# A hybrid attention block: the input projection as fp16 halves with scales made on the chip

## The chip, the cores and the metric

The kernel runs on one core of one Trainium2 chip. The metric is the device time of one execution in microseconds, as the median of several runs; an execution is also profiled, and its trace gives the span from the first to the last instruction and the place of each instruction on each engine: PE (TensorE), DVE (VectorE), ACT (ScalarE), POOL (GpSimd) and SP (SyncE, which here issues DMAs). PEld is the loading of PE's weights.

## The reference

One layer of a decoder block on 16 meta tokens and 512 real ones, width 1024, all in float32. Two attention branches of 16 heads each, MLA and forgetting attention ("fox"), read one common input projection:

```
u = rmsnorm(h, pre_norm_g)
cq, ckv, k_pe_raw, z_mla, fq, fk, fv, f_logit, z_fox, gate_a, gate_b = split(u @ w_in)
q  = rmsnorm(cq) @ w_uq ; kv = rmsnorm(ckv) @ w_ukv ; rope on q_pe and k_pe
o_mla = causal_attention(q_m, k_m, v_mla)
cum = cumsum(log_sigmoid(f_logit + fox_forget_b))
o_fox = causal_attention(fq, fk, fv, cum)          # logit[t,s] += cum[t] - cum[s]
y_mla = (o_mla * silu(z_mla)) @ w_br_mla ; y_fox = (o_fox * silu(z_fox)) @ w_br_fox
mixed = (sigmoid(gate_a) * y_mla + sigmoid(gate_b) * y_fox) @ w_out
out = h + rmsnorm(mixed, post_norm_g)              # without the meta tokens
```

## The kernel before

**Split products.** A float32 product is made of three matmuls in the type fp32r: high times high, high times low, low times high. Each operand X is split into a high part (a cast, on ScalarE) and a low part (X minus the high part, on GpSimd or VectorE). `passes` issues the three for each slice of 128 of the contraction. The normed input, transposed, stands in `uTh` and `uTl`.

**Units.** The input projection is cut into units of 128 output columns: q, k and v of a pair of fox heads (PE's fq, fk, v), z of each branch, and the gates (pg). A unit of 512 tokens is 24 matmuls of 512 columns; k and v, with the meta tokens, are 48 matmuls, 24 of 272 and 24 of 256 columns. The weights of a unit come by one DMA of 512 KB into `wraw` (`wload`), are split by `wsplit` (the cast is L136; the low part L105, on the engine that `low[0]` names, mostly GpSimd) and go to PE. `weights` returns the getter, `ahead` ties the load of a unit to a place some units earlier.

**Stages.** The opening (0 to 59 us) norms and transposes the input, makes the small latent projection (psm), q and k of the first fox pair, the rotary part (ppe), v and half a gate. Sixteen attention stages follow, for each of eight pairs of heads first fox, then MLA. A stage on PE is: scores (st), the product of the stage before with its values (ov), and a fill of projection units for later stages. A fox stage fills with z of fox, then z of MLA in three pieces, with the MLA query and key-value units (mq, mk, v from the latents, fp32r) between the pieces; an MLA stage fills with fq, fk and v of the next fox pair. While PE runs the fill, VectorE evicts the scores with the bias and the running maximum (L795; for fox with `cbp` and its masked copy `cbm`, which come back by DMA from `c_dram`, the scan of the forget gates), ScalarE takes exponentials (L830) and makes the high part of the normed probabilities (L865), VectorE their low part (L869), GpSimd the short meta part (L850 to L855), all into `pn`. A transposing DMA brings `pn` to `pt`, and `ov` uses `pt` with the values, in fp16, two heads side by side. The last stage fills with three gates. A merge follows (407 to 490 us: fox's branch product as a Strassen-like set x, y, z, with two gates between its sets), then MLA's branch product (py) with the last gate, the output projection and the norm.

**Order.** PE's order in the attention stages is written by hand in the fills. The other engines take their instructions in the order of a scheduler that goes by priority and dependence; `tc.issue_after` and `keep_in_program_order` pin some of them.

Of the kernel before, what the change touches and what calls it, by code (L numbers as in the profile page):

```python
# [11 lines left out]
F32 = mybir.dt.float32  # L12
# [26 lines left out]
SC_FOX = 1.0 / math.sqrt(HD)  # L39
# [8 lines left out]
ROW = 64  # L48
# [7 lines left out]
def block_kernel(ctx: ExitStack, tc: tile.TileContext, x, meta_tokens, pre_norm_g, w_in, fox_forget_b,  # L56
# [19 lines left out]
    uT0 = [const.tile([128, KD, ROW + L - META], F32R, tag=n, name=n) for n in ("uTh", "uTl")]  # L76
    uTh, uTl = (t[:, :, ROW - META :] for t in uT0)
# [29 lines left out]
    def wload(srcs):  # L107
# [3 lines left out]
        raw = wp.tile([128, 1024], F32, tag="wraw", name=f"wraw{u}")  # L111
# [13 lines left out]
    low = [nc.gpsimd]  # L125

    def room_of(u, up=0):
        w = wp.tile([128, 2112], F32R, tag="w", name=f"w{u}")
        return [w[:, o + up : o + up + 1024] for o in (0, 1024)]

    def wsplit(ld, up=0):

        u, raw, parts, n = ld
        wh, wl = room_of(u, up)
# [9 lines left out]
    def weights(srcs, wrap, up=0):  # L144
# [11 lines left out]
        return get  # L156

# [23 lines left out]
    def unit(name, getw, act, nk, sls, done, banks=None):  # L181
# [26 lines left out]
        if hasattr(getw, "load"):  # L208
            out[0][1].load = getw.load
        return out  # L210
# [5 lines left out]
    def u_act(k):  # L216
        return uTh[:, k, :], uTl[:, k, :]
# [7 lines left out]
    def win_w(off, i, up=0):  # L225
        return weights(lambda: [win[:, :, off + 128 * i : off + 128 * i + 128]], lambda w: by_k(w[0], KD), up)
# [14 lines left out]
    def hl_done(key, n, w):  # L241

        def done(i, ps):
# [6 lines left out]
            with tc.high_priority(offset=30), tc.issue_after(normed[0]) if key == ("q", 0, 0) else nullcontext():  # L250
                halved[key, i] = nc.scalar.copy(hl[:, 0, o : o + w_], ps).ins
            with tc.high_priority(offset=30):
                lowered[key, i] = split_lo(nc.vector, hl[:, 1, o : o + w_], ps, hl[:, 0, o : o + w_]).ins
        return done

    def q_fox(pr):
        return unit(f"fq{pr}", win_w(O_FQ, pr), u_act, KD, REAL, hl_done(("q", 1, pr), S, S))

    def k_fox(pr):
        return unit(f"fk{pr}", win_w(O_FK, pr, UP), u_act, KD, ALLT, hl_done(("k", 1, pr), L, HALF), keybank[0])  # L260
# [4 lines left out]
    with ExitStack() as ph:  # L265
# [56 lines left out]
        fT = pal.tile([NH, L], F32, tag="fT", name="fT")  # L322
# [4 lines left out]

        hns, sts, pts0, squared = {}, {}, {}, {}
# [58 lines left out]

        psms = {}
# [14 lines left out]
        def back(t):  # L403
# [19 lines left out]
            for a, b, i in both:  # L423
                nc.vector.scalar_tensor_tensor(out=sm[:rows, a:b], in0=psm[:rows, a:b], scalar=st2[:rows, 2 + i : 3 + i],
                                               in1=gq[:rows, a:b], op0=ALU.mult, op1=ALU.mult)
# [27 lines left out]
        tps(gps[:, 0, 0:KD], g8, ident[0:KD, 0:KD])  # L453
        squares(0, pin)
        scaled(0, pin)
        pin(nc.vector.tensor_copy(gcol, gps[:, 0, 0:KD]))
# [943 lines left out]
```

## Time and profile before

| | |
|---|---|
| median of 3 runs | 585.56 us (585.5 to 585.57) |
| the profiled execution | 585.71 us |
| its span | 583.5 us |
| opening | 0 to 59 us |
| 16 attention stages | 59 to 407 us |
| merge with gates | 407 to 490 us |
| branch product of MLA, output projection, norm | 490 to 583.5 us |

The span is shorter than the time of the execution by what lies around the first and the last instruction. The page gives the busy time of each engine, which is an average over these parts; its chain of work goes back from the last instruction to whatever released each step, so that it names what sets the end.

### The profile page before, as it was taken

To read this page: it belongs to the slowest core of one execution; us is meant where nothing else is said; L and a number is where in the kernel's file an instruction comes from. 1 tells how busy PE (TensorE), PEld (TensorE's weight loads), DVE (VectorE), ACT (ScalarE), POOL (GpSimd) and SP (SyncE) were. 2 spreads that over 40 slices of the span, in tenths; PEclk is the share of its full clock that TensorE was granted. 3 is DMA by queue.
4 is the path that set the end of the run, shared out by engine and by line. 5 is a ranking of instruction groups with operands and counts; after the bars stand their busy time and mean duration, and the time that the engine had idled before them with its cause. 6 is when DMAs were issued, how large, how long until landed. Compare 5 with 4: busy or idle time off the path is not lost.

```text
span 583.5 us, 11105 instructions
## 1 busy us (share of the span) xinstructions
PE 574.2 (98%) x3841; PEld 496.5 (85%) x3841; DVE 414.5 (71%) x1156; ACT 356.4 (61%) x816; POOL 200.7 (34%) x270
## 2 busy tenths in 40 slices
PE   8999999999999999999999999999999999999995
PEld 6989889889889888888898898878998998888884
DVE  5854876884775775767758748895747876468967
ACT  7856774884774775767748747944343462443762
POOL 4317835464468472654544634520000000000000
PEclk9999999999999999999999999999999999999999
DMA  9535699999978999988987978977722534332603
GB/s 293 119 88 151 125 189 218 234 184 269 175 167 158 231 192 215 220 164 208 186 175 182 216 158 147 184 168 259 210 73 72 145 105 132 89 110 88 237 0 144
DMA packets 219999, 97.46 MB, mean 167 GB/s; under 512 B 131456, under 2 KB 209672, under 8 KB 219944
## 3 DMA queue, kind: packets, MB, share of 16 engines
q1 hardware_dynamic: 219944, 96.77, 71.2%
q8 instruction: 30, 0.49, 0.3%
q14 instruction: 25, 0.20, 0.1%
HBM read 62.36 MB, written 3.97 MB: 114 GB/s over the span
## 4 chain that ended last, share of the span: by engine, by line
PE 93%; ACT 2%; DMA 2%; issue 1%; POOL 1%; SPq 0%; DVE 0%; DVEq 0%; ACTq 0%; POOLq 0%
PE z L99 17%; PE pg L99 15%; PE v L99 9%; PE fk L99 8%; PE fq L99 8%; PE x L99 8%; PE py L99 7%; PE st L99 7%; PE ov L99 5%; PE psm L99 3%; PE y L99 2%; PE mq L99 2%; DMA pt<-pn 1%; PE ppe L99 1%; DMA wsr<-in_w_in_dram 1%; PE mk L99 1%
## 5 line engine op out<-in xcount | busy, mean ns | idle before, releaser
L105 POOL TENSOR_TENSOR w<-wraw,w 128x1024 fp32r<-128x1024 f32 (+2 forms) x61 | 118.6, 1951 | 113.8 <-ACT w L136 81.5
L136 ACT CAST w<-wraw 128x1024 fp32r<-128x1024 f32 (+1 forms) x72 | 74.6, 1041 | 48.5 <-PE py L99 19.7
L99 PE MATMUL z<-uTh,w 128*128 128x512 f32 x256 | 85.0, 393 | 0.0
L99 PE MATMUL pg<-uTh,w 128*128 128x512 f32 x256 | 80.7, 391 | 0.0
L830 ACT ACTIVATE sf<-sf,nb 128x272 f32<-128x272 f32 (+3 forms) x128 | 72.7, 569 | 11.5 <-DVE nb L795 10.6
L105 DVE TENSOR_TENSOR w<-wraw,w 128x512 fp32r<-128x512 f32 (+1 forms) x55 | 51.6, 949 | 27.9 <-ACT w L1125 20.0
L869 DVE SCALAR_TENSOR_TENSOR pn<-sf,ri,pn 128x512 f16<-128x512 f32 (+3 forms) x128 | 69.6, 609 | 1.6 <-ACT pn L865 1.5
L865 ACT ACTIVATE pn<-sf,ri 128x128 f16<-128x128 f32 (+3 forms) x128 | 59.7, 548 | 0.5 <-DVE ri L835 0.5
L99 PEld LDWEIGHTS pg<-uTh,w 128*128 128x128 f32 x256 | 48.1, 188 | 10.2 <-issue 0.3
L99 PEld LDWEIGHTS z<-uTh,w 128*128 128x128 f32 x256 | 48.1, 188 | 10.2
L99 PE MATMUL z<-uTl,w 128*128 128x512 f32 x128 | 50.1, 391 | 0.0
L99 PE MATMUL pg<-uTl,w 128*128 128x512 f32 x128 | 49.9, 390 | 0.0
L99 PE MATMUL fk<-uTh,w 128*128 128x272 f32 (+1 forms) x256 | 48.5, 283 | 0.0
L99 PE MATMUL v<-uTh,w 128*128 128x272 f32 (+1 forms) x256 | 47.5, 283 | 0.0
L99 PE MATMUL fq<-uTh,w 128*128 128x512 f32 x128 | 42.0, 398 | 0.0
L99 PE MATMUL st<-hlk,hlq 64*128 64x272 f32 (+4 forms) x480 | 41.2, 299 | 0.0
L710 DVE TENSOR_REDUCE vsc<-v 128x1 f32<-128x272 f32 (+1 forms) x32 | 13.2, 433 | 39.5 <-PE v L99 39.5
L99 PEld LDWEIGHTS fk<-uTh,w 128*128 128x128 f32 x256 | 40.4, 188 | 0.3
L99 PEld LDWEIGHTS v<-uTh,w 128*128 128x128 f32 x256 | 40.0, 188 | 0.1
L99 PE MATMUL py<-gh,w 128*128 128x512 f32 x128 | 39.7, 389 | 0.0
L99 PEld LDWEIGHTS st<-hlk,hlq 64*128 64x128 f32 x480 | 33.1, 186 | 4.1 <-ACT vh L729 2.8
L99 PE MATMUL v<-uTl,w 128*128 128x256 f32 (+1 forms) x128 | 36.2, 283 | 0.0
(255 smaller groups left out, 1332.1 us busy)
## 6 DMA issues: line engine op xcount, KB each, us to landing
wraw<-in_w_in_dram SPq DMA_DIRECT2D x56, 512.0 KB, 4.8
cbp<-c_dram SPq DMA_DIRECT2D x16, 264.0 KB, 4.0
wraw<-in_w_br_fox_dram SPq DMA_DIRECT2D x8, 512.0 KB, 4.2
tb<-in_w_out_dram SPq DMA_DIRECT2D x8, 512.0 KB, 5.4
wraw<-in_w_br_mla_dram SPq DMA_DIRECT2D x8, 512.0 KB, 4.2
wraw<-in_w_out_dram SPq DMA_DIRECT2D x6, 512.0 KB, 4.2
xr<-in_x_dram SPq DMA_DIRECT2D x4, 512.0 KB
out_dram<-yo SPq DMA_DIRECT2D x8, 256.0 KB, 2.0
```

The source lines that it names most:

```text
L99: nc.tensor.matmul(*a, **k)
L105: return eng.tensor_tensor(out=lo, in0=src, in1=f32(hi), op=ALU.subtract)
L136: nc.scalar.copy(wh[:, :n], raw[:, :n])
L710: nc.vector.tensor_reduce(out=sc[:, i : i + 1], in_=ps, op=ALU.max, axis=AX.X, apply_absolute_value=True)
L830: exps[b // 3] = nc.scalar.activation(sf, sf, AF.Exp, bias=sums["nb"][:, h, b : b + 1], scale=-1.0, accum_out=sums["su"][:, h, b : b + 1]).ins
L865: normed[:] = [nc.scalar.activation(hi, sf, AF.Copy, scale=rib).ins]
L869: nc.vector.scalar_tensor_tensor(out=lo, in0=sf, scalar=rib, in1=hi, op0=ALU.mult, op1=ALU.subtract)
```

## The change

All units of the input projection, except the first fox q, k and v and the first gate (`plain_w`), become objects of a class `Halved`: their weights are multiplied by a power of two s per unit and held as two fp16 halves, and the input is held as fp16 halves `hTh`, `hTl` beside `uTh`, `uTl`. PE still does three matmuls for each slice of the contraction. What was scaled is scaled back in the operations that read the result (`.r`: the scale of tanh, of the eviction in `hl_done`, of v's factor `vsc`).

For each unit one instruction takes the largest magnitude of each partition (Abs with a running sum as a bound on ScalarE, L198, or a reduction on VectorE, L200), one stage ahead of the conversion. For each set of two or three units a matmul of 1 to 3 columns with a constant 128x128 tile `spread` brings the sum over partitions to all of them, VectorE cuts it to a power of two and inverts it (L213, L215), GpSimd makes `.r` (L216). The high half is then one activation with a scale (L255), the low half two instructions on GpSimd (L260, L261) or one on VectorE (L258).

```diff
+    def scales(ws):
+        def peak(j):
...
+            if on[0] is nc.scalar:
+                    tc.keep_in_program_order(nc.scalar.activation(junk[0], raw, AF.Abs, accum_out=mp))
+            else:
+                tc.keep_in_program_order(nc.vector.tensor_reduce(out=mp, in_=raw, op=ALU.max, axis=AX.X, apply_absolute_value=True))
+        def run_():
...
+            mm(ps, spread, sc[:, 0:2].bitcast(BF16)[:, 0:n], start=True, stop=True)
...
+                nc.vector.tensor_scalar(out=t.bitcast(I32), in0=ps.bitcast(I32), scalar1=0x7F800000, scalar2=0x00800000,
+                                        op0=ALU.bitwise_and, op1=ALU.bitwise_or)
+                nc.vector.reciprocal(inv, t)
+                nc.gpsimd.tensor_scalar(out=r, in0=t, scalar1=su[:, 5:6], scalar2=1.0, op0=ALU.mult, op1=ALU.mult)
...
+    class Halved:
...
+            room = wp.tile([128, 1088], F32R, tag="w", name=f"w{u}", bufs=4)
+            hi, lo = (room.bitcast(F16)[:, o : o + 1024] for o in (0, 1024))
...
+                self.hi = nc.scalar.activation(hi, raw, AF.Copy, scale=self.s).ins
...
+                if low[0] is nc.vector and not self.pool:
+                    nc.vector.scalar_tensor_tensor(out=lo, in0=raw, scalar=self.s, in1=hi, op0=ALU.mult, op1=ALU.subtract)
+                else:
+                    nc.gpsimd.tensor_scalar(out=raw, in0=raw, scalar1=self.s, scalar2=1.0, op0=ALU.mult, op1=ALU.mult)
+                    self.lo = nc.gpsimd.tensor_tensor(out=lo, in0=raw, in1=hi, op=ALU.subtract).ins
...
     def u_act(k):
-        return uTh[:, k, :], uTl[:, k, :]
+        return hTh[:, k, :], hTl[:, k, :]
...
+        def narrowed(t, after):
...
+            with tc.issue_after(squared[3]):
+                nc.scalar.activation(hTh[:, :, ts], f32(uTh[:, :, ts]), AF.Copy, scale=su[:, 2:3])
...
+                for out, u, op, x in ((rest, uTh, ALU.subtract, hTh[:, ks, ts]), (hTl[:, ks, ts], uTl, ALU.add, rest)):
+                    with tc.issue_after(after):
+                        nc.vector.scalar_tensor_tensor(out=out, in0=f32(u[:, ks, ts]), scalar=su[:, 2:3], in1=x, op0=ALU.mult, op1=op)
...
+        for t in (4, 0, 1):
+            narrowed(t, lowered["sm", 3])
         run(qk[7:])
+        for t in (2, 3):
+            narrowed(t, lowered[("k", 1, 0), t - 2])
...
-                fill = vts[br, pr] + q + k[:KD] + v + k[KD:]
+                    fill = vts[br, pr] + q + k[:KD] + v[:4] + call(ws[0].scale, ws[0]) + v[4:8] + call(lambda n=si + 1: peaks(sets[n][2:], nc.vector)) + v[8:] + call(ws[1]) + k[KD:]
```

Other edits make room: the split weights of what stays fp32r take two tiles (`w`, `wl`) of two pools, loads run through more buffers and further ahead (`wraw2`, `wb`), the tiles of the attention results (`gT`) take the place of `uTh` and `uTl`, the merge gets rooms of its own for the gates' weights, and the second rotary unit stands seven steps later in its fill. In the merge every second gate's low half is made on VectorE.

On PE, a piece of the order in the middle of a fox stage's fill, before. The rows are matmuls of z of fox and the first of mq, the MLA query unit; an fp32r matmul is one instruction with its weights.

```order
L99 MATMUL z_1529<-uTh,w_1524 128x512 x2
L99 MATMUL z_1529<-uTl,w_1524 128x512
L99 MATMUL z_1529<-uTh,w_1524 128x512
L99 MATMUL mq_1593<-cTh,w_1579 128x512
L99 MATMUL mq_1593<-cTl,w_1579 128x512
```

The same fill in the change, at the middle of z of fox and at its end. `spread` and `scale_1658` belong to the scales of the next pair's q, k and v.

```order
L104 LDWEIGHTS spread
L104 MATMUL scale_1658<-sc_1388,spread 128x3
L104 LDWEIGHTS w_1435
L104 MATMUL z_1619<-hTh,w_1435 128x512
...
L104 MATMUL z_1619<-hTh,w_1435 128x512
L104 MATMUL mq_1684<-cTh,w_1679 128x512
L104 MATMUL mq_1684<-cTl,w_1679 128x512
```

Weights of the fp16 units are loaded by instructions of their own, a small matmul with a load of `spread` stands inside z, and where mq begins, fp16 gives way to fp32r, as it does at each border between a z piece and the MLA units.

On POOL, the weights that are split during one fox stage, before (`vsc` is a tiny factor of v):

```order
L105 TENSOR_TENSOR w_1785<-wraw_1527,w_1785 128x1024
L105 TENSOR_TENSOR w_1846<-wraw_1584,w_1846 128x1024
L720 TENSOR_SCALAR vsc_1647<-vsc_1647 128x1
L105 TENSOR_TENSOR w_1900<-wraw_1600,w_1900 128x1024
L850 TENSOR_TENSOR mt_1864<-sf_1681,ri_1679 128x32
```

And in the change, for the same stage:

```order
L216 TENSOR_SCALAR sc_1388<-sc_1388,su 128x3
L260 TENSOR_SCALAR wraw_1091<-wraw_1091,sc_1388 128x1024
L261 TENSOR_TENSOR w_1758<-wraw_1091,w_1758 128x1024
L260 TENSOR_SCALAR wraw_1093<-wraw_1093,sc_1388 128x1024
L261 TENSOR_TENSOR w_1775<-wraw_1093,w_1775 128x1024
L886 TENSOR_SCALAR vsc_1740<-vsc_1740 128x1
L260 TENSOR_SCALAR wraw_1095<-wraw_1095,sc_1388 128x1024
L920 TENSOR_SCALAR vsc_1740<-sc_1385,vsc_1740 128x1
L261 TENSOR_TENSOR w_1932<-wraw_1095,w_1932 128x1024
L1020 TENSOR_TENSOR mt_1965<-sf_1789,ri_1787 128x32
```

Each low half has a pass over the raw weights ahead of its subtraction; the first meta operation of the next stage's probabilities (`mt`) stands behind them as before.

On ACT, the opening from the first high part of q (`hlq`) to the last table load, before. `fa` is the forget gate, the casts into `w` are weights: `w_777` is v of the first pair.

```order
L251 CAST hlq_618<-fq_578 128x512
L520 ACTIVATE fa<-fT 16x528
L136 CAST w_777<-wraw_733 128x1024
L521 ACT_TABLE_LOAD
L521 ACTIVATE fa<-fa 16x528
L251 CAST hlk_651<-fk_626 128x272
L522 ACT_TABLE_LOAD
L522 ACTIVATE fa<-fa 16x528
L251 CAST hlk_651<-fk_654 128x256
```

The same piece in the change, from the input's halves on; v's cast is `w_824` now, and `w_777` is the rotary unit's.

```order
L522 ACTIVATE hTh<-uTh,su 128x8x128 x3
L582 CAST cTh<-pc_616 128x3x128
L583 CAST KPH<-pc_616 32x128
L584 ACTIVATE fT<-pc_616,fb 16x128
L376 ACTIVATE hlq_646<-fq_594,eps_t 128x512
L671 ACTIVATE fa<-fT 16x528
L162 CAST w_777<-wraw_772 128x512
L672 ACT_TABLE_LOAD
L672 ACTIVATE fa<-fa 16x528
L376 ACTIVATE hlk_680<-fk_655,eps_t 128x272
L673 ACT_TABLE_LOAD
L673 ACTIVATE fa<-fa 16x528
```

Behind the last of these rows stand v's cast `w_824` and then the second half of `hlk`. On DVE the fourteen passes of L530 that make `hTl` and its rests stand between the operations of the opening, the last five of 512 elements between the low half of `hlk` and the scan of the forget gates.

More of the change, by code (lines that the diff above doesn't have):

```diff
@@ L985, in block_kernel @@
         lctx.close()
-        gpool = gctx.enter_context(tc.tile_pool(name="gpool", bufs=1, side="right"))
-        gT += [gpool.tile([128, KD, S], F32, tag=n, name=n) for n in ("gT0", "gT1")]
-        run(opening[len(pe0) : -4])
-        behind[:] = [halved[("k", 1, 0), 1]]
+        for w in first_z:
+            w.room = lambda: more[0].tile([128, 1024], F32, tag="wraw2", name=f"wraw{uid[0]}")
+            w.load()
+            w.peak()
+        behind[:] = [squared[3]]
+        run(opening[len(pe0) : len(pe0) + KD])
+        behind[:] = [halved[("k", 1, 0), 1]]
+        g[0][1].prep()
+        first_z[0].scale()
+        first_z[0]()
+        run(opening[len(pe0) + KD : -4])
+        cycle[0] = 7
+        for w in sets[0]:
+            w.load()
         run(opening[-4:])
@@ L1210, in block_kernel @@
             split_to(S2, g11)
[L1211 to L1213 removed]
+            next(pairs[0])
+        run(after[1])
+        with tc.issue_after(sets[-1][1].hi):
             split_to(A12, g12)
```

329 lines of the change are left out of this document (256 added, 73 removed).

## The prediction

> **What bounds the kernel now.** I read the page first: the busy share of each engine, the clock row, and the chain of work that ended last.
>
> ```profile
> PE 574.2 (98%) x3841; PEld 496.5 (85%) x3841; DVE 414.5 (71%) x1156; ACT 356.4 (61%) x816; POOL 200.7 (34%) x270
> PEclk9999999999999999999999999999999999999999
> PE 93%; ACT 2%; DMA 2%; issue 1%; POOL 1%; SPq 0%; DVE 0%; DVEq 0%; ACTq 0%; POOLq 0%
> ```
>
> PE is busy nearly throughout at full clock, and 93% of the chain is PE. Next the waits of PE by what ended them; these are the longest and the last.
>
> ```profile
> PE spun L99 <- DVE KPL L238: 1.4, 1, 1.4
> PE ov L99 <- DMA pt<-pn: 0.3, 1, 0.3
> ```
>
> Both lie early; after the first ov, PE waits for nobody. So a microsecond of stream removed behind that ov is a microsecond of span, as long as no other engine falls behind; and what is removed ahead of it counts only if that ov comes earlier as well. The profiled execution took 585.71 us for a span of 583.5; the 2.2 us around it stay. The median of the three runs, 585.56, is 0.15 us lower, so the sum is made on 585.7 and rounded.
>
> **The stream.** The order of PE gives the matmuls that turn fp16: 912 of 512 columns (z 384, pg 360, fq 168), and 336 each of 272 and of 256 (fk, v). Their pace today, from the chain (start, us, what):
>
> ```profile
> 98.38 2.72 PE fk L99 x24
> 105.25 5.66 PE z L99 x24
> 112.28 2.04 PE z L99 x9
> 130.39 3.04 PE fk L99 x24
> 438.07 10.90 PE pg L99 x48
> ```
>
> 10.90/48 = 227 ns for 512 columns, 3.04/24 = 126.7 for 272, 2.72/24 = 113.3 for 256. What fp16 costs is seen in ov, which runs two heads side by side on 64 columns of weights each. Five narrow windows of PE's timeline in one ov; the first column is the start of the first pair in flight.
>
> ```profile
> 103.67 0.60 PE L99 MATMUL ov<-pt,vp 128*64 128x512 f16 x4
> 103.89 0.55 PE L99 MATMUL ov<-pt,vp 128*64 128x512 f16 x4
> 104.10 0.49 PE L99 MATMUL ov<-pt,vp 128*64 128x384 f16 x4
> 104.70 0.39 PE L99 MATMUL ov<-pt,vp 128*64 128x256 f16 x4
> 104.81 0.39 PE L99 MATMUL ov<-pt,vp 128*64 128x256 f16 x6
> ```
>
> From 103.67 to 104.10 two pairs of 512 start: 215 ns each; the pair of 256 takes 109 or 110. For 272 I interpolate 116. The saving is 912 x 12.1 ns = 11.0 us, 336 x 10.7 = 3.6, 336 x 4 = 1.3 to 1.4: **-16 us**. No full 128-column fp16 weight stands in the trace; if it gave nothing this would be 0, and there is no row by which it would give more.
>
> **Switches and scale matmuls.** fp16 units now alternate with fp32r ones. In a pair of stages z, mq, z, mk, z, mv, z changes type six times (48 in eight pairs), and ppe and the merge add about 18: 66. No row has fp16 beside fp32r in the same tile shape. The nearest are a change of matmul mode in the opening, and the start of z after ov, which changes type and tile.
>
> ```profile
> 36.11 4.80 PE fq L99 x21
> 40.92 0.44 PE pc L102 x4
> 41.35 0.70 PE fq L99 x3
> ```
>
> The 24 fq and 4 pc take 5.94; 24 x 0.227 leaves 0.49 for four 128-column transposes, which alone could fill 0.44: 0.05 per round trip, 0.03 per switch. The upper end is z: 5.66 - 24 x 0.227 = 0.21. So 66 switches cost 0 to 14 us; only the type changes here, so I take 0.03: **+2 us**. The 23 scale matmuls (128x128 weights, 1 to 3 columns) cost between 0 and the 109 ns of 256 columns; half: **+1.3 us**. The start of z after ov may fall too, since both are fp16 now: 0 to -0.2 at each of 15 places; I take 0.
>
> **The helpers inside a pair of stages.** A pair is a fox and an mla stage; this one is typical (the columns are PE, PEld, DVE, ACT, POOL busy):
>
> ```profile
> 228.44:269.25 40.81, 40.81 (x321) 35.43 (x322) 28.69 (x105) 28.13 (x70) 20.66 (x30) 1.00 0.94 206
> L345 ACT ACTIVATE hn<-ht x4: 1044/1060/1062, 6.8 to 17.6; 128x1024 f32<-128x1024 f32 x3, 16x1024 f32<-16x1024 f32 x1
> L345 ACT ACTIVATION_READ_ACCUMULATOR hn<-ht x4: 183/184/187, 7.8 to 18.6; 128x1 f32 x3, 16x1 f32 x1
> L710 DVE TENSOR_REDUCE vsc<-v x32: 423/433/443, 53.6 to 364.8; 128x1 f32<-128x272 f32 x16, 128x1 f32<-128x256 f32 x16
> ```
>
> PE's pair shortens to about 40.81 - 1.6 (48 z and 24 fq at 12.1 ns, 48 at 10.7, 48 at 4) + 0.2 + 0.1 = 39.5. ACT gets two maxima of 1.06 + 0.18: 30.6. The hi conversions replace casts of the same 1024 elements. DVE gets three reductions; 433 ns for 272 elements scales to at most 1.6 for 1024, and four tiny scale operations (0.2 each): 34.4. Both fit. POOL's low halves become two instructions, a TENSOR_SCALAR of 128x1024 (time T) and the old TENSOR_TENSOR; five units a pair, so 5T + about 1.3 for tiny ones: **22 + 5T**. T is not in the trace. Rows near it, with the median or mean in ns:
>
> ```profile
> L306 POOL CAST wsh<-wsr x3: 904/912/962, 8.2 to 10.7; 128x864 fp32r<-128x864 f32 x3
> L523 POOL TENSOR_SCALAR fa<-fT x1: 1994/1994/1994, 42.5 to 42.5; 16x528 f32<-16x528 f32 x1
> L105 POOL TENSOR_TENSOR w<-wraw,w x61: 728/2387/3747, 24.2 to 381.7; 128x1024 fp32r<-128x1024 f32 x43, 128x256 fp32r<-128x256 f32 x16, 128x512 fp32r<-128x512 f32 x2
> L869 DVE SCALAR_TENSOR_TENSOR pn<-sf,ri,pn x128: 344/605/2744, 67.8 to 378.1; 128x128 f16<-128x128 f32 x32, 128x256 f16<-128x256 f32 x32, 128x384 f16<-128x384 f32 x32, 128x512 f16<-128x512 f32 x32
> L869 DVE SCALAR_TENSOR_TENSOR pn<-sf,ri,pn 128x512 f16<-128x512 f32 (+3 forms) x16 | 8.5, 598 | 0.2 <-ACT pn L865 0.2
> ```
>
> One-input CAST: 912 x 1024/864 = 1.1 us. The same operation, but mult then max on 16 partitions: 1994 x 1024/528 = 3.9. I take T near the cast, 1.1 to 1.5, because there too one tensor is read and one written and the width matches; that is a choice between far ends, and the first rival takes the other. POOL is then about 29 of 39.5 and hidden. For engines that all run fuller I add **+1 us** (0 to 5).
>
> [...]
>
> **The opening.** Here PE's stream is not all that counts. ACT must now also make hTh (five operations, 4224 elements a partition, 4.5 us by the 1060 row), ahead of the last cTh; DVE makes hTl in two passes of 8448 elements, some 10 us; and v0's weight cast, which stood ahead of the table loads, stands behind them. Rows of ACT's, POOL's and DVE's timelines and of the chain (start, us):
>
> ```profile
> 41.39 0.48 ACT L438 CAST cTh<-pc 128x384 fp32r<-128x384 f32 x1 [3.00 <-PE pc L102]
> 43.46 1.03 ACT L136 CAST w<-wraw 128x1024 fp32r<-128x1024 f32 x1
> 48.02 0.65 ACT L522 ACTIVATE fa<-fa 16x528 f32<-16x528 f32 x1
> 46.46 2.40 POOL L105 TENSOR_TENSOR w<-wraw,w 128x1024 fp32r<-128x1024 f32 x1
> 50.57 5.77 PE v L99 x48
> 48.57 0.34 ACT L251 CAST hlk<-fk 128x256 fp32r<-128x256 f32 x1
> 48.78 0.70 DVE L524 SCALAR_TENSOR_TENSOR fa<-fa 16x528 f32<-16x528 f32 x1 [1.59 <-ACT fa L522]
> 49.74 1.24 DVE L527 TENSOR_TENSOR_SCAN fa<-fa 16x528 f32<-16x528 f32 x1
> 57.63 0.20 POOL L924 COPY cbm<-cbp 128x16 f32<-128x16 f32 x1 [0.70 <-DMA cbp<-c_dram]
> 60.03 0.31 DVE L795 CUSTOM_DVE_ANT_0 sf<-st,cbp 128x144 f32<-128x144 f32 x1 [0.60 <-PE st L99]
> 74.89 6.82 DMA pt<-pn
> 81.85 2.04 PE ov L99 x26
> ```
>
> hTh fits into the 3.0 idle and a little before, and is about 0.8 late. Without the 1.03 cast but with ppe's 0.6 in its place, Ln ends about 0.4 later than 48.67, so v0's cast ends near 50.1 and POOL's low half near 52.5. PE wants that low half with its third v matmul, at 50.8: a stall of about 1.7. Behind the wait stand pg and the scores. On DVE the scan stands behind four more passes of hTl: hlk's cast (0.34) ends about 50.4, then its low half (0.4), five passes of 512 elements (0.7 each, as L524) and the scan, ending near 55.5 instead of 50.98. Its c goes out by DMA and returns as cbp 6.6 us later, near 62, where the first evictions read cbp at 60.03. They start about 2 to 3 us late; maximum, pn, transpose DMA and the first ov follow in a line. PE has work only until 81.5, so it waits. The two delays overlap: **+3 us** (0 to 6). The fp16 saving ahead of that ov (gate and z work, 48 x 12 ns) only fills this wait: **+0.6**.
>
> Sum: 585.7 - 16 + 2 + 1.3 + 1 + 3 + 0.6 = 577.6; I say **578**. Its own range, with small terms at either end, is 570 to 584.
>
> **Rivals.** (1) POOL becomes the bound, which ends slower. With T = 3.9 POOL has 22 + 19.5 = 41.5 in a pair of 39.5: 0.7 above today's 40.81. And the maxima of L105 and L869 above (3747, 2744 against 2387, 605) show that operations of DVE and POOL that read two SBUF tensors wait for each other; POOL then reads nearly always, so up to 8.5 more per pair is added. Seven pairs: 585.7 + 5 to + 64, less about 4 saved in the merge: 587 to 646, likeliest near 610. It decides from T = (39.5 - 22)/5 = 3.5 with no collisions and 1.8 with all. For it: L523. Against: the cast. Chance 0.20.
>
> [...]
>
> (2) Every switch costs what z's start costs: 66 x 0.2 = 13 instead of 2, 589; slower. For it: no row has such a switch. Against: the fq, pc round trip. Chance 0.06. (3) The change does not do what it says, because 128-column fp16 weights load no faster than they are used: stream 0, 593. Against: ov loads two fp16 weights per 109 ns. Chance 0.04. (4) Other engines' lateness eats the gain (a maximum or a scale waits behind pn in ACT's or DVE's queue, 0.5 us a stage): 585.7, no change. Speaking for it: DVE at 87%. Chance 0.08.
>
> **How the numbers follow.** Forecast 0.62. A difference under 0.2% (1.2 us) is what a measurement of this kernel can tell from none. Faster: 0.62 + 0.02 from weak forms of the rivals = 0.64. Same: rival 4 and a little of 1 = 0.10. Slower: 0.26. The range takes the forecast's lower end and reaches up through rivals 2 to 4 and the mild half of 1: 570 to 603, leaving out about 0.15.
>
> **What would show it.** z x24 at about 5.3, fk at 2.8 and 2.6, pg x48 at 10.4. L260's mean on POOL is T; PE idle in the pairs with releaser POOL w is rival 1. z x9 pieces between mq and mk well over 1.95 are rival 2. A PE wait at v for POOL wl near 51 and at the first ov for pt is the opening. I am wrong if PE has waits in every pair, or if the first ov stands beyond 88.

## The result: slower, and where the time went

The changed kernel takes 601.92 us (median of 4 runs, 600.39 to 605.57) beside 585.53 us for the kernel before on the same chip (585.3 to 585.57): a ratio of 1.029, 95% interval 1.0244 to 1.0336. The forecast was 578; the sign was wrong. The profiled execution took 601.86 us.

The page of the changed kernel, first the lines that answer to those shown before: busy time, granted clock in 40 slices, and the chain by engine.

```profile
PE 571.5 (95%) x3864; PEld 404.9 (67%) x3864; DVE 479.8 (80%) x1243; ACT 393.8 (66%) x861; POOL 280.0 (47%) x364
PEclk9999797979999999989999999999999999999999
PE 79%; DVE 8%; DMA 5%; ACT 3%; issue 2%; POOL 2%; SPq 0%; DVEq 0%; POOLq 0%; ACTq 0%
```

PE is busy 2.7 us less than before, but its share fell from 98 to 95%; the chain, 93% PE before, now runs for 8% over DVE and 5% over DMA. The clock row has dips in slices 5, 7 and 9 (15 us each, so from 60 to 135 us); before it had none. A smaller one stands in slice 18 (255 to 270 us). The waits of PE by what ended them (total, times, longest):

```profile
PE ov L104 <- DMA pt<-pn: 11.5, 4, 5.1
PE x L104 <- ACT gT L1409: 2.5, 1, 2.5
PE v L104 <- POOL wl L110: 1.8, 1, 1.8
PE pg L104 <- POOL w L261: 1.6, 1, 1.6
PE st L104 <- DVE vh L898: 1.3, 1, 1.3
PE st L104 <- DVE pt L824: 0.6, 1, 0.6
```

Idle gaps of PE from 45 us on add up to 20.7 us; before, to 0.3. They stand in three places: 12.5 us up to the second ov (1.83, 0.60, 1.35, 3.70 and 5.06), 2.8 at the ov of 182 and 266 (0.58 and 2.18), and 5.3 from the gates of the last stage on, most of it at the start of the merge. The chain (start, us, what) through the first two stages, and at the ov of 266, shows the rest:

```profile
87.30 5.61 DMA pt<-pn
92.95 3.84 PE ov L104 x26
96.79 6.34 PE fq L104 x24
103.14 2.78 PE fk L104 x24
...
115.00 6.08 DMA pt<-pn
121.21 3.84 PE ov L104 x26
125.05 3.29 PE z L104 x12
128.34 2.61 PE z L104 x12
132.35 1.96 PE z L104 x9
...
144.53 5.29 PE fq L104 x24
...
265.65 3.39 PE ov L104 x26
```

ov took 2.04 before; behind the two long waits it takes 3.84, behind that of 266 3.39, the fq that follows the first 6.34 instead of 5.29, and z x12 3.29 instead of 2.61 to 2.70. The granted clock shows why. Five windows of the changed kernel (the columns are PE, PEld, DVE, ACT, POOL busy; then granted clock, DMA share, GB/s):

```profile
64.80:71.50 6.70, 5.98 (x16) 4.58 (x17) 3.85 (x23) 3.29 (x12) 6.16 (x10) 0.50 0.74 208
92.10:98.80 6.70, 5.84 (x31) 2.86 (x32) 3.52 (x8) 3.80 (x10) 6.55 (x13) 0.50 1.09 302
119.50:126.10 6.60, 4.89 (x29) 2.81 (x30) 1.52 (x9) 1.75 (x7) 0.04 (x1) 0.50 1.09 311
266.20:269.50 3.30, 3.30 (x26) 2.20 (x22) 0.60 (x2) 1.95 (x6) 2.26 (x8) 0.50 1.14 346
205.00:245.00 40.00, 40.00 (x332) 27.13 (x330) 36.27 (x117) 31.58 (x75) 30.70 (x40) 1.00 0.95 182
```

In the first four PE runs at half its clock. They hold twelve gate matmuls that should take 2.75 us (12 x 0.229, their pace before) and take 4.9, the first two ov with what follows them, and most of the ov of 266. PE is busy for 20.0 us in these four; at full clock that work would have taken about half, so the lower clock costs about 10 us (an estimate from the busy times and the clock of 0.50).

So the account closes: 20.3 us more idle and 10 us of lower clock against a last matmul that starts 16.6 us later (593.86 against 577.23). That leaves about -14 for the stream, where -16 + 2 + 1.3 was forecast. **What was removed is gone; the waits are new.** The starts in us of what lies between the opening and the end, read from PE's timeline:

| start of | before | after | later by |
|---|---|---|---|
| first v matmul | 50.41 | 50.53 | 0.1 |
| first ov | 81.85 | 92.95 | 11.1 |
| second ov | 103.21 | 121.21 | 18.0 |
| sixth ov | 187.56 | 205.35 | 17.8 |
| eighth ov | 228.37 | 244.51 | 16.1 |
| last ov | 391.52 | 404.98 | 13.5 |
| merge, first x | 407.22 | 421.54 | 14.3 |
| first py | 490.42 | 507.17 | 16.75 |

From the sixth to the eighth ov the pair is 1.65 us shorter, as meant. The 18 us are lost ahead of the second ov; 3.9 more go at the ov of 266 (a wait of 2.18, then half clock), and 3.3 from the last ov to py.

How the first ov came to be late can be followed on DVE and POOL (start, us, engine, line; the last bracket is idle time and what ended it):

```profile
50.82 5.26 DVE L530 SCALAR_TENSOR_TENSOR rest<-uTh,su,hTh 128x512 f32<-128x512 f32 x2
50.27 5.27 POOL L110 TENSOR_TENSOR wl<-wraw,w 128x1024 fp32r<-128x1024 f32 x2
58.00 1.24 DVE L682 TENSOR_TENSOR_SCAN fa<-fa 16x528 f32<-16x528 f32 x1
59.88 0.67 DVE L824 TENSOR_TENSOR pt<-ppe,pt 128x512 f32<-128x512 f32 x1
```

Two passes that take 1.4 us alone (the next two: 56.01, 1.40) take 5.26 while POOL makes the two low halves `wl`, of v0 and the first gate. The scan starts 8.3 us later than before (49.74), the rotary products 9.0 (50.90). From there the lateness changes as it goes: first eviction 65.68 (+5.7), pn complete 81.05 (+8.5), last transpose of stage 0 issued 87.30 (+12.4), first ov +11.1. From pn complete to the last transpose it is 6.25 us, 2.3 before; what adds these 4 us stands on SP's own queue, of the changed kernel and then of the one before:

```profile
76.80 4.33 SPq L98 DMA_DIRECT2D QP<-gT  x7
81.24 5.09 SPq L98 DMA_TRANSPOSE pt<-pn  x3
...
87.30 3.62 SPq L98 DMA_TRANSPOSE pt<-pn  x1
90.96 5.78 SPq L98 DMA_DIRECT2D wraw<-in_w_in_dram  x5
96.78 3.15 SPq L98 DMA_DIRECT2D qpe_dram<-gT  x4
100.04 3.04 SPq L98 DMA_TRANSPOSE vp<-vh  x1
103.13 4.05 SPq L98 DMA_DIRECT2D qpe_dram<-gT  x4
107.35 0.79 SPq L98 DMA_DIRECT2D QP<-qpe_dram  x1
108.25 10.09 SPq L98 DMA_TRANSPOSE pt<-pn  x4
```

```profile
61.49 6.12 SPq L93 DMA_DIRECT2D QP<-gT  x8
...
68.97 9.30 SPq L93 DMA_TRANSPOSE pt<-pn  x4
...
90.48 8.85 SPq L93 DMA_TRANSPOSE pt<-pn  x4
...
120.19 3.35 SPq L93 DMA_DIRECT2D qpe_dram<-gT  x4
```

The writes of the rotary result (QP<-gT) stand before the transposes in both, and now come 15 us later. In stage 1 five weight loads, two groups of stores and QP stand ahead of the transposes: pn is complete at 103.5, the transposes begin at 108.25. The second group of stores stood behind stage 2's transposes before (120.19).

At the merge DVE and POOL collide again. POOL, changed kernel:

```profile
399.10 1.12 POOL L260 TENSOR_SCALAR wraw<-wraw,sc 128x1024 f32<-128x1024 f32 x1 [1.25 <-ACT w L255]
400.31 2.14 POOL L261 TENSOR_TENSOR w<-wraw,w 128x1024 f16<-128x1024 f32 x1
402.42 6.26 POOL L260 TENSOR_SCALAR wraw<-wraw,sc 128x1024 f32<-128x1024 f32 x2
408.65 6.15 POOL L261 TENSOR_TENSOR w<-wraw,w 128x1024 f16<-128x1024 f32 x2
```

The same two operations that took 1.12 and 2.14 take 3.13 and 3.08 each while DVE splits the merge's operands, and DVE's of 1.21 take up to 3.14 in the same stretch.

### The profile page after: what moved, and what is told of

It is laid out like the page before. It is cut to its first block, busy times and chain, and to the rows that moved or that the text cites. A ratio compares the mean times of both kernels' runs of the same rounds, so it can differ in the third digit from the quotient of the medians.

```text
span 600.1 us, 11346 instructions
## 1 busy us (share of the span) xinstructions
PE 571.5 (95%) x3864; PEld 404.9 (67%) x3864; DVE 479.8 (80%) x1243; ACT 393.8 (66%) x861; POOL 280.0 (47%) x364
## 4 chain that ended last, share of the span: by engine, by line
PE 79%; DVE 8%; DMA 5%; ACT 3%; issue 2%; POOL 2%; SPq 0%; DVEq 0%; POOLq 0%; ACTq 0%
PE z L104 16%; PE pg L104 10%; PE py L104 7%; PE v L104 7%; PE fq L104 6%; PE fk L104 6%; PE x L104 6%; PE ov L104 6%; PE st L104 6%; DMA pt<-pn 4%; PE psm L104 3%; PE mq L104 2%; DVE rest L530 2%; PE y L104 2%; POOL w L261 1%
## 5 line engine op out<-in xcount | busy, mean ns | idle before, releaser
L104 PEld LDWEIGHTS <-w 128*128 128x128 f16 x1584 | 150.3, 98 | 117.2 <-issue 6.2
L261 POOL TENSOR_TENSOR w<-wraw,w 128x1024 f16<-128x1024 f32 x42 | 91.9, 2188 | 2.6
L104 PE MATMUL z<-hTh,w 128*128 128x512 f16 x256 | 82.3, 382 | 0.0
L104 PE MATMUL pg<-hTh,w 128*128 128x512 f16 x240 | 72.6, 379 | 2.4 <-POOL w L261 1.6
L255 ACT ACTIVATE w<-wraw,sc 128x1024 f16<-128x1024 f32 x43 | 48.3, 1144 | 24.6 <-DVE sc L215 18.0
L260 POOL TENSOR_SCALAR wraw<-wraw,sc 128x1024 f32<-128x1024 f32 x42 | 51.8, 1235 | 26.2 <-ACT w L255 24.0
L216 POOL TENSOR_SCALAR sc<-sc,su 128x2 f32<-128x2 f32 (+2 forms) x22 | 8.3, 379 | 91.4 <-DVE sc L213 91.4
L104 PE MATMUL z<-hTl,w 128*128 128x512 f16 x128 | 48.8, 381 | 0.0
L104 PE MATMUL ov<-pt,vp 128*64 128x512 f16 (+4 forms) x416 | 37.6, 338 | 11.5 <-DMA pt<-pn 11.5
L104 PE MATMUL pg<-hTl,w 128*128 128x512 f16 x120 | 45.5, 379 | 0.0
L104 PEld LDWEIGHTS <-vp 128*64 128x64 f16 (+1 forms) x416 | 24.2, 120 | 26.8 <-issue 14.3
L104 PE MATMUL fk<-hTh,w 128*128 128x272 f16 (+1 forms) x224 | 40.1, 276 | 0.0
L162 ACT CAST w<-wraw 128x1024 fp32r<-128x1024 f32 (+1 forms) x20 | 20.2, 1014 | 16.9 <-PE py L104 15.3
```

Of the source, the lines that this page charges most:

```text
L104: nc.tensor.matmul(*a, **k)
L162: nc.scalar.copy(wh[:, :n], raw[:, :n])
L216: nc.gpsimd.tensor_scalar(out=r, in0=t, scalar1=su[:, 5:6], scalar2=1.0, op0=ALU.mult, op1=ALU.mult)
L255: self.hi = nc.scalar.activation(hi, raw, AF.Copy, scale=self.s).ins
L260: nc.gpsimd.tensor_scalar(out=raw, in0=raw, scalar1=self.s, scalar2=1.0, op0=ALU.mult, op1=ALU.mult)
L261: self.lo = nc.gpsimd.tensor_tensor(out=lo, in0=raw, in1=hi, op=ALU.subtract).ins
```

## The experiments

"Shift" is how much earlier (-) or later (+) a matmul starts than in the changed kernel: first ov, second ov, last matmul of the kernel. Ratios are to the kernel before, measured beside each run. Each version ran two to four times, and one version's times lie up to 7.8 us apart (the changed kernel's own 5.2); a shift is read from one execution. So a difference of 2 or 3 us between two versions is not told from this scatter, unless the trace shows the wait that went or came.

### Narrowing, collision, or both

The first run leaves out the low half of the narrowed tokens (GpSimd sets hTl to zero early): DVE's fourteen passes are gone, and no other work.

```
-            for ks in (slice(0, KD),) if t not in (2, 3) else (slice(0, 4), slice(4, KD)):
+            for ks in ():
```

> The fourteen passes on VectorE that make the low half of the fp16 input are left out (hTl is set to zero once, early on GpSimd), so the input's low half does not enter the fp16 units; all matmuls stay. Theory A (VectorE's new work in the opening holds the scan, the rotary products and v's factor, and with them the first scores): the first scores of PE start near 59.5 instead of 61.5 and run without the wait of 1.35, the first ov starts near 84 instead of 92.95 and the whole comes to about 588 us instead of 601.9. Theory B (the transposes of the probabilities stand late in SyncE's queue, whatever VectorE does): the first ov gains at most 4 us, the second ov keeps its wait of about 5 us, and the whole stays above 594. Rival C (the loss comes from maxima and conversions in all stages): no more than 2 us gained.

596.19 us, 1.0176 [1.0108, 1.0244]; shifts -4.55, -5.72, -7.25. The passes cost about this much, but 3.27 and 3.77 us of wait were left at the first two ov, and 1.34 at v.

The second run leaves out the low halves of v0's and the first gate's weights instead (the high half is used three times), so POOL has no such work while DVE makes its last passes.

```
+            if only:
+                return [(wh[:, o : o + w], wh[:, o : o + w]) for o, w in parts]
```

> The low halves of the weights of the first v and the first gate are not made: these two units multiply by the high half a third time, so the two GpSimd subtractions of 2.4 us at 50.3 to 55.5 are gone and all matmuls stay. If VectorE was held by those two (two passes of 512 took 5.19 us instead of 1.4), the same passes take 1.4 us, the first ov starts about 4 us earlier (near 89) and the wait of 1.83 us at v is gone; total about 597. If VectorE and GpSimd do not hold each other, the passes stay at 5.2 us, and only the wait at v goes, total 600 or more.

596.62 us, 1.0183 [1.0136, 1.023]; shifts -4.45, -4.57, -4.24; the wait at v is gone too. The two passes that had taken 5.26 us in this run:

```profile
51.13 1.39 DVE L532 SCALAR_TENSOR_TENSOR rest<-uTh,su,hTh 128x512 f32<-128x512 f32 x2
```

DVE did the same work as in the changed kernel, so the collision, with that wait, is worth 4.2 to 4.6 us. The two costs lie on one line and overlap, as the run with both left out (and 4, 10 and 14 idle matmuls, see below) shows:

> The low half of the fp16 input and the low halves of the first v's and the first gate's weights are left out together, and idle matmuls (4, 10 and 14) stand at the first scores and the first two ov. If VectorE's new passes, the two GpSimd subtractions and the clock are the whole loss of the opening, the first ov comes at 84 to 85 and the total falls to about 586. If something else holds stage 0 (the rotary products behind the shared space of uT and gT, and SyncE's queue), the first ov stays at 87 to 88 and the total at 590 or more.

593.71 us, 1.0145 [1.0104, 1.0186]; shifts -5.99, -6.39, -7.17: at the end no more than the first alone, by these traces (the medians lie 2.5 us apart). The first ov still starts 5.1 us and the second 11.6 us later than before. Something else holds them.

### The granted clock

Idle matmuls on PE (their result is not read) fill the waits at the first two ov, to hold the clock up.

```
+            if si in (1, 2):
+                spin = ov_bank(f"spin{si}")
+                for _ in range((16, 22)[si - 1]):
+                    mm(spin, hTh[:, 0, 0:128], hTh[:, 0, META:L], start=True, stop=True)
```

> Sixteen matmuls of 512 columns without use stand on TensorE ahead of the first ov and twenty-two ahead of the second, into the bank that ov overwrites. They only fill the waits of 3.7 and 5.06 us. If the granted clock falls because TensorE pauses, ov takes 1.97 us again instead of 3.84 in both places, fq after the first ov 5.3 instead of 6.34 and z after the second 5.3 instead of 5.9, and the total is about 5 us lower, near 597. If the clock falls for another reason, the total stays within 2 us of 601.9.

598.89 us, 1.0222 [1.0192, 1.0252], mean clock 0.991 instead of 0.978; shifts -1.08, -2.18, -3.08. With 12 more ahead of stage 0's scores:

> As with the idle matmuls ahead of the first two ov, and twelve more ahead of the first scores, where TensorE waits for v's evictions; nothing is left out. If most of what the opening loses is the clock that falls behind each pause (mean 0.87 from 65 to 142 us), the clock stays above 0.97 there, the gate's second half takes 2.7 us instead of 5.0 and the first ov comes near 90; total near 594. If the clock is a small part, the total stays where the sixteen and twenty-two alone had it, near 599.

598.9 us, 1.0233 [1.0204, 1.0263]; shifts +1.10, -0.41, -2.46. Twelve more brought nothing; that idle matmuls themselves take part of what they save is argued, not measured. Idle matmuls won back some 3 us of the 10. Not all of that is theirs: in the trace with 16 and 22 the clock stayed at 1.00 behind pauses of 0.55 and 1.35 us that stand ahead of them, where in the changed kernel 0.60 and 1.35 had brought it down. The lower clock follows the waits: in the changed kernel each of its four stretches begins in one or just behind one (64.8, 92.1, 119.5 and 266.2).

### Order on DVE, POOL and SP

DVE: scan and rotary products ahead of the last eight passes.

```
+        for t in (2, 3):
+            narrowed(t, turned_pe[-1], 2)
```

> Order of VectorE alone in the opening: the scan of the forget gates and the four rotary products come ahead of the passes that make hTl of the last two blocks of tokens (eight passes of 512); nothing is left out. If the place of the passes holds the first scores, the wait of 1.35 inside the first scores goes, VectorE's evictions start near 62 instead of 65.7 and the first ov near 89; total about 597. If their sheer length holds them (no slack before z), the passes come late instead, z of the first pair waits for hTl by 2 to 4 us and the total stays within 2 us of 601.9.

602.15 us, 1.0283 [1.0253, 1.0313]; shifts -1.50, -1.56, +0.12. What the scan gained, the reductions of v behind the passes lost: the scan starts at 51.44 instead of 58.00, the first eviction at 66.27 instead of 65.68.

SP: the stores of heads 4 to 8 behind stage 1's transposes (before, they stood behind stage 2's), and the next pair's bias behind stage 0's:

```
-                if si == 2:
+                if si == 3:
                     stores(4, 8)
```

> Order of SyncE's queue alone, without touching the loads of the second pair: the four stores of pairs 2 and 3 behind the transposes of stage 1, and the copy of the next bias behind the fourth transpose of stage 0. The last transpose of stage 0 is issued about 1 us earlier and those of stage 1 about 4 us earlier; the waits at the first two ov shrink from 3.7 and 5.06 to about 2.8 and 1; total about 597. If the queue is not what holds them, the waits stay.

600.49 us, 1.0255 [1.0217, 1.0292]; shifts -2.00, -3.04, -0.68; 5.25 us of wait left at the second ov. Both orders together:

> The two orders together, nothing left out. If the two causes add up, the first ov comes near 88 and the second without a wait; total near 592, still above the kernel before, since the passes themselves and the later weights remain.

600.73 us, 1.0259 [1.0164, 1.0354]; shifts -1.69, -2.46, +1.15: no sum of the two. In another, those stores and the weight loads for two stages ahead were put behind stage 1's transposes; its edit also held back the MLA weights (w_uq at 113.37 instead of 71.33):

> Order of SyncE's queue alone: the four stores of the rotary queries of pairs 2 and 3 go back behind the transposes of stage 1, and the three loads of the second pair's q, k, v stand behind those transposes too. Theory B: the transposes of stage 1 are issued about 8 us earlier (near 100 instead of 108.25), the second ov has no wait instead of 5.06 us, and the clock does not fall there; total about 594. Theory A alone: the wait at the second ov only shrinks with the opening, so it stays near 5 and the total within 2 us of 601.9.

604.26 us, 1.0314 [1.0218, 1.0409]. The wait at the second ov went, and one of 7.72 us came at the scores of stage 2 (second ov +2.53). I first read this as the delayed load of w_uq; the two runs at the end, which load w_uq early, show the same stop. POOL: the masked bias ahead of the first z weight's low half.

```
+        held[:] = [masks[0]]
         first_z[0]()
+        held.clear()
```

> The changed kernel with one edge added on POOL: the scaled low half of the first z weight (L260, L261, which stand at 61.97 to 65.83) is put behind the masked bias (L1094, L1095, at 67.06). Theory P (POOL's queue order holds the first softmax): the masked bias comes near 63, the first pn are complete 1 to 3 us earlier than 81.05, the first ov starts 1 to 3 us earlier than 92.95, total 599 to 601. Theory D (only the length of DVE's passes and their collisions hold it): first ov within 0.5 us, total 601.5 to 602.5.

600.77 us, 1.0282 [1.0227, 1.0337]; shifts -0.23, -0.39, -0.49 (four runs, 599.34 to 607.09): no gain from POOL's order here.

### The start of the merge

The low halves of the last stage's units on DVE instead of POOL:

```
             sc, n0, n1, va = attention(br, pr)
+            if last:
+                low[0] = nc.vector
```

> The low halves of the weights of the four units at the end of the last stage are made by VectorE in one instruction (1.3 us each) instead of GpSimd's two; nothing is left out. If GpSimd and VectorE hold each other there (GpSimd takes 12.4 us for two low halves, VectorE 2.6 and 3.1 us for operations of 1.2), the waits of 1.63 us at the gate and of 2.54 us at x go and the total falls by 3 to 4 us, to about 598. If the merge is late for the maxima or the room of the weights, the waits stay.

596.45 us, 1.0192 [1.0162, 1.0221]. Up to the last ov 1.24 us are gained, to the first py 5.66: 4.4 us lie in between, and the waits of 1.6 and 2.5 are gone. One engine doing both in turn is quicker here than two that stop each other: the three low halves take DVE 3.68 us, and its splits their 1.2 again.

### The maxima

A fixed scale of 64; no maximum, no reduction, no scale matmul.

```
             raw = ws[j].load()[1]
+            return
```

> No unit's maximum is taken and no scale is worked out: all units use one fixed scale of 64 and its factor back; conversions, halves and all other matmuls stay. Twenty Abs on ScalarE, 32 reductions and 44 tiny operations on VectorE and 22 scale matmuls are gone. If the maxima hold the merge (chain through the reductions of 1.2 us between VectorE's sums there), the merge loses its waits of 1.6 and 2.5 us and gains about 5 us, and the transposes of stage 7 and of stage 1, which wait behind ScalarE and POOL, come about 2 us earlier: total near 594. If they are hidden, only the scale matmuls go (about 1.5 us): total 600.

608.03 us, 1.0384 [1.0354, 1.0414]; shifts +2.42, +1.49, +5.69. Leaving work out made it slower, with 14.5 us of wait at ov (11.5 in the changed kernel), 5.2 at pg for a weight and 3.5 at the first scores. So what the maxima cost can't be priced by taking them out; why it came out slower was not followed.

### All that helped, and what is left

Order on DVE, SP's stores, bias and QP behind stage 1's transposes, 12, 12 and 14 idle matmuls, and the merge's low halves on DVE:

> All orders together with nothing left out: scan and rotary products ahead of the last passes of hTl, the four stores, the next bias and the next rotary queries behind the transposes in SyncE's queue, idle matmuls at the first scores and the first two ov (12, 12, 14), and VectorE for the low halves at the end. If the causes found so far are the loss, the second ov has a wait under 1 us, the clock stays above 0.98 and the total comes to 585 to 590. If it stays above 595, a cause is missing.

593.42 us, 1.014 [1.0032, 1.0248]; shifts -2.89, -5.55, -11.19. It is the fastest version that was found that leaves nothing out, and still slower than before (two runs, 590.76 and 596.09; the trace is of the first). Its granted clock is 0.997 over the span, without the four slow stretches. From the second ov on it gains 7.0 us on the kernel before (12.45 late there, 5.44 at the end). With POOL's order added:

> e12 with the same edge. Theory P: first ov 1 to 2 us earlier than e12's 90.06, total 591 to 592.5. Theory D: as e12, 593 to 594.

598.63 us, 1.0225 [1.0207, 1.0244]; shifts +0.81, -1.50, -1.98. z now waits 2.1 us for its low half. Then the early cast of v0's weight, the halves of two token blocks later, and fewer idle matmuls:

> e14, and v0's weight cast ahead of the forget gate's table loads again, so that POOL makes its low half before 50; the fp16 halves of token blocks 2 and 3 (two ACT operations, eight DVE passes) behind ppe's rotary products and the gate's cast; 0, 8 and 8 idle matmuls instead of 12, 12, 14. Theory O (what is left of the loss is the length of the opening's work on ACT, POOL and DVE ahead of the first eviction): no wait at v near 51, scan ended by 53, first ov 3 to 5 us earlier than e12's, total 586 to 590. Theory Q (the SP queue and the rotary results that wait for the gate hold stages 0 and 1 whatever the opening does): first ov at most 1.5 us earlier than e14's, total 591 to 593.

602.62 us, 1.0278 [1.0231, 1.0325]; shifts +6.40, +5.17, +3.72. The wait at v is gone, and the passes now stand between the steps of v's scaling on DVE: the scores wait 4.62 and 1.29 us for vh. Wherever the passes go, something on DVE that PE needs soon is behind them. How far it would go without them: low halves left out as above (all fourteen passes), SP and merge as in the best version, POOL's order too, 0, 8 and 8 idle matmuls.

> The low half of the narrowed tokens (DVE's ten passes) and the two low halves of v0's and the first gate's weights on POOL are left out, as in e10, but with the SP queue and the last stage as in e12, the POOL edge of e13, and 0, 8 and 8 idle matmuls. It is the floor of what curing the opening can bring. Theory O: first ov within 2 us of before's 81.85, second within 3 us of 103.21, total 578 to 584, faster than before. Theory Q: second ov still 6 to 10 us later than before, total 587 to 592.

593.12 us, 1.0133 [1.0117, 1.0149]; first ov 86.75 (+4.9 on before), second 113.94 (+10.7). The opening is nearly cured in this run (no wait at v, the first scores at 60.54 against 59.02 before) and stages 0 and 1 are still late: my theory that its length was all falls. SP's queue in it:

```profile
72.07 4.32 SPq L98 DMA_DIRECT2D QP<-gT  x7
76.49 8.69 SPq L98 DMA_TRANSPOSE pt<-pn  x4
...
86.04 6.86 SPq L98 DMA_DIRECT2D wraw<-in_w_in_dram  x5
92.94 2.57 SPq L98 DMA_DIRECT2D qpe_dram<-gT  x4
95.61 3.07 SPq L98 DMA_TRANSPOSE vp<-vh  x1
...
99.49 2.80 SPq L98 DMA_TRANSPOSE pt<-pn  x1
...
103.71 8.14 SPq L98 DMA_TRANSPOSE pt<-pn  x3
```

pn of stage 0 is complete at 74.3, 1.8 us later than before, but its transposes begin 7.5 us later, right behind the writes of the rotary result. POOL makes that result at 66.75 to 70.5 (before 60.85 to 64.7): it now makes the first z weight's low half among its steps (1.13 and 2.14 us; POOL's order in this run puts it there, in the changed kernel it stands ahead of them), and since gT lies where uT lay, nothing could be written there before the gate's matmuls end, at 65.8; in the changed kernel POOL stood idle 1.06 us for that. In stage 1 the transposes begin 9 us later than before's 90.48, behind the loads, the stores and vp.

So the last two runs put the stores and the three loads for two stages ahead behind stage 1's transposes, once in the best version and once in the bare one:

```
+                if si == 1:
+                    hold[:] = turned_in[-1:]
+                    late_load[0] = True
+                    stores(2, 4)
+                    for w in sets[2]:
+                        w.load()
```

> e12, and on SP's queue the four stores of the rotary result (qpe_dram, 94 to 97) and the three weight loads for two stages ahead (87 to 93) behind stage 1's four transposes instead of ahead of them; 12, 12 and 8 idle matmuls. Theory Q (those seven issues stand before the transposes and hold the second ov): stage 1's transposes are issued 5 to 8 us earlier than in e12, no wait at the second ov, second ov 2 to 4 us earlier than e12's 115.66, total 589 to 592. Theory D (the first ov's delay alone, passed on through DVE, sets the second): transposes wait for pn, second ov within 1 us of e12's, total 592.5 to 594.5.

> e16 (narrowed low half and the two low halves of the opening left out) with SP's queue as in e17; 0, 8 and 4 idle matmuls. Theory Q: stage 1's transposes are issued from about 95 instead of 99.49 and 103.71, second ov 4 to 6 us earlier than e16's 113.94, total 586.5 to 589. Theory D: second ov within 1 us, total 592 to 594.

603.49 us, 1.0303 [1.0277, 1.0329], and 602.0 us, 1.0266 [1.0237, 1.0295]. In the bare version the transposes end at 106.4 instead of 111.9 and in both there is no wait for them at the second ov, yet it starts 13.5 us later than in the best version, and 12.4 later than in the bare one. DVE's timeline and SP's queue in the first of them:

```profile
103.76 0.44 DVE L880 TENSOR_REDUCE vsc<-v 128x1 f32<-128x272 f32 x1 [0.95 <-PE v L104]
117.98 1.22 DVE L203 TENSOR_REDUCE sc<-wraw 128x1 bf16<-128x1024 f32 x1 [13.78 <-DMA wraw<-in_w_in_dram]
119.12 0.42 DVE L880 TENSOR_REDUCE vsc<-v 128x1 f32<-128x256 f32 x1
```

```profile
107.78 2.59 SPq L98 DMA_DIRECT2D qpe_dram<-gT  x4
110.41 5.87 SPq L98 DMA_DIRECT2D wraw<-in_w_in_dram  x3
```

DVE stands still for 13.78 us at a weight's maximum (L203) whose load is now late, and behind it in DVE's order stand v's second reduction and the low half of the keys that PE's scores need. Neither theory's number came. Their common assumption, that those loads can wait, is wrong: **because each maximum stands a stage ahead in DVE's order, its load must stand further ahead still on SP, in front of the transposes.** The earlier run with those loads moved had the same stop, 7.22 us. The stores alone behind the transposes, with the loads left in front, were not tried.

## Why the prediction was wrong, step by step

**The stream** was right. pg x48 takes 10.38 (forecast 10.4), z x9 1.96 (1.95), fk 2.78 and 2.62 (2.8 and 2.6), fq x24 5.29 (z x24 was put at 5.3). mq between z's takes 1.39 to 1.41 instead of 1.36: two switches cost 0.03 to 0.05 there, no more than the 0.03 each that was chosen. A steady pair is 1.65 us shorter (1.3 forecast), and the whole stream gives the -14 above against -12.7. Rivals 2 and 3 are out.

**T and the helpers** were right too. POOL's group by line:

```profile
L260 POOL TENSOR_SCALAR wraw<-wraw,sc 128x1024 f32<-128x1024 f32 x42 | 51.8, 1235 | 26.2 <-ACT w L255 24.0
```

T is 1.24 us (1.1 to 1.5 chosen; 3.9 by the far row). In the pair from 205 to 245 POOL is busy 30.7 us (29 forecast), ACT 31.6 (30.6), DVE 36.3 (34.4) of 40. No helper became the bound, so rival 1 as priced, 610 through every pair, is out. The fuller engines' +1 (0 to 5) measured 2.8 of wait at 182 and 266, and 4.5 with the slow clock behind the second; what made those two transposes late was not followed.

**The opening's +3 (0 to 6) is the step that failed.** The first ov is 11.1 us late instead of 3; the bound that I set, 88, was passed by 5. Three things in that sum were wrong. (1) It priced DVE's passes at 0.7 each, while rival 1 said, from two maxima of before (3747 and 2744 ns), that DVE's and POOL's two-input operations wait for each other, and the opening's own paragraph put POOL's low half at that very time (the stall of 1.7 at v that it forecast measured 1.8). The effect was there and was counted only for steady pairs, where it cost little (POOL 30.7 us busy, 29 forecast); in the opening it is worth 4.2 to 4.6 us with the wait at v, and at the merge up to 4.4, where POOL's own two steps went as well. In the opening 1.4 us of DVE's passes took 5.26 beside 5.27 of POOL, and at the merge two L260 of 1.12 took 6.26 beside DVE's splits. L260 reads one tensor of 128x1024, not two, and was held all the same. (2) It followed the forget gate's scan to the first eviction ("about 2 to 3 us late"; measured 5.7) but not what stands behind it on DVE: the rotary products (9.0 late), then v's scaling. (3) It stopped at pn. The rotary result goes to QP over the same SP queue ahead of the transposes, and it comes late itself, behind DVE's products, POOL's new work and the gate. Even with narrowing and low halves out, that leaves 4.9 us at the first ov. This last reading is from the trace of that run, where the issues follow each other without a gap; a version with gT elsewhere was not tried.

**Stage 1 had no term at all**, and lost 6.9 us more (5.06 of wait and about 3 of clock, less what the stream gained). The step was "after the first ov, PE waits for nobody", read from the trace of before and carried over to a kernel whose loads, stores and maxima stand elsewhere. Each issue on SP's queue that the change moved was to be counted and was not. Rival 4 had the mechanism (a maximum that waits in DVE's queue) with 0.5 us a stage; in the changed kernel it shows as the order of SP that it forces, and in the two last runs as the stop itself, 13.78 us.

**The clock** was taken as constant, because the clock row of before showed no dip. But that row belongs to a PE without pauses. About 10 us of the loss are matmuls at half the clock behind a pause; the sum had no term for it.

**The merge's start** was not in the sum. From the last ov to py 3.3 us were lost, and 4.4 came back when the low halves went to DVE.

**The range.** That 601.92 lies inside 570 to 603 is luck. Its upper end was drawn for costs that would come back in every pair, and the steady pairs got shorter; the time was lost in the opening, in stage 1 and around the merge.

What stays open: how much of the second ov's lateness is SP's order by itself. Moving the issues only moved the stop, and a version in which both the loads are early and the transposes free (another queue for the loads) was not tried. Nor is it settled why the kernel without maxima is slower.

## What to carry to other kernels

A bound of 98% PE says what a faster stream can give at most; it says nothing of the stages where the pipeline fills. Here one late result went on from queue to queue there: the scan 8.3 us late on DVE, the last transpose of stage 0 12.4 on SP, the first ov 11.1 on PE. When a change puts new work on DVE and POOL at once, price DVE's passes beside POOL's work on weights as if the two ran in turn, at that place: here 1.4 us of DVE's became 5.26 in the opening, and POOL's 1.12 became 3.13 at the merge. When a job that waits for a load is moved a stage ahead, count its load on the DMA queue too, and what that load now stands in front of.

## What the runs showed of the hardware

- The granted clock fell behind short pauses. In the changed kernel it was 0.50 from 64.8 to 71.5 us, where pauses of 0.60 and 1.35 us lay 1.7 us apart and the second was not yet over (a gate matmul of 512 columns then starts every 427 ns instead of 229), and from 266.2 to 269.5 behind one of 2.18. In the pauses of 3.70 and 5.06 us the clock was down by 92.1 and 119.5, 2.8 and 3.35 us after PE stopped. The length of a pause didn't settle it alone: behind 2.50 us at 424.7 the clock stayed at 1.00. What else does was not tested.
- With full 128-column fp16 weights a matmul of 512 columns started every 216 ns (pg x48 in 10.38 us), of 272 every 116 and of 256 every 109 (fk x24 in 2.78 and 2.62), where fp32r took 227, 126.7 and 113.3.
- By the medians, the version with idle matmuls in two pauses was 3 us faster, and the one without work on ACT, DVE and PE (the maxima) 6 us slower.
